# A hybrid decoder layer whose instructions are ordered by the scheduler's timeline model instead of its default estimate

## The chip, the cores and the metric

The kernel runs on one core of a Trainium2 chip. The core has a matmul engine (TensorE; PE in the profile, with its weight loads as a row PEld), a vector engine (DVE), an activation engine (ACT), a general engine (POOL), and a queue that issues the transfers (SP). Each engine takes its instructions strictly in the order in which the program gives them, and an instruction that depends on another engine waits for a semaphore. The metric is device microseconds for one execution; lower is better.

## The reference, cut to what matters

The computation is one layer over x of shape (1, 2048, 1024) in float32, and a final RMSNorm:

```python
h = _rmsnorm(x, norm_w[l])
proj = h @ w_in[l]                       # 8456 columns, split in 13 pieces
y_a = _hgrn2_branch(a_q, a_f, a_i, a_g, lb_all[l], norm_a[l])            # gated linear recurrence, 4 heads
y_b = _gated_deltanet_branch(b_qkv, b_z, b_beta, b_a, conv_w[l], ...)    # delta rule, 4 heads
y_c = _swa_sink_branch(c_q, c_k, c_v, c_g, sinks[l], bias_blk)           # windowed attention, 8 heads
lifted = jnp.einsum('bsnc,ncd->bsnd', ys, w_branch[l])
gates = jax.nn.sigmoid(gate_logits.reshape(Bn, S, N_BRANCHES, D_MODEL))
x = x + jnp.sum(gates * lifted, axis=2) @ w_out[l]
return _rmsnorm(x, final_norm)
```

The delta rule needs, for each chunk, the inverse of a lower triangular matrix with ones on its diagonal (`triangular_solve(eye + A, eye)`), and then carries a 128x128 state from chunk to chunk.

## The kernel before, in words

The sequence is worked through in four blocks of 512 positions (`block(s, ...)`), each with the same program. Two kinds of matmul stand in it.

**Dense matmuls.** Every projection, every lift of a branch and the output projection splits its operands in a high and a low part and makes three matmuls per 128 rows of the contraction: lines 101, 102, 103 (function `mm_ct`, 512 columns each, 24 for one projection, into one of four PSUM banks `ps_d`), or lines 169, 170, 171 (`mm_tc`). Their weights come through `load_w` into four buffers `wHL`: in the first block from the inputs with a split on ACT and DVE (lines 86, 87), later from a copy kept in DRAM (line 82, `wHL<-kept`, 512 KB for twelve matmuls). Dense matmuls of one unit depend little on other units, so they can stand between the small matmuls of another.

**Small matmuls.** Each block has four units A (`unit_a`, lines 402 to 446), four units B (`unit_b`, lines 512 to 645) and four units C (`unit_c`, lines 694 to 732), on the PSUM banks `ps_c0` and `ps_c1`. They are chains: a few small matmuls, then work on DVE, ACT or by DMA on their result, then the next small matmuls. A float32 matmul stands in the trace as two records. In a unit B the chain is:

- line 547: scores of the four chunks, four matmuls in two pairs; DVE makes `NTt` and `QKT` of them (550, 552); ACT copies the diagonal blocks of all four chunks to `NS` (566)
- the inverse of 32 blocks of 16x16, which takes a way through DRAM in both directions:

```python
566  A.copy(NS[r:r + 64], NTt[r:r + 64, :, r:r + 64])
567  nc.sync.dma_start(half(sN, r), NS[r:r + 64])
570  nc.sync.dma_start(L, diag(sN))
574  V.tensor_tensor(t3, ...)                      # 14 steps of two operations on DVE
576  V.tensor_tensor(L[:, 0:j, j + 1:16], ...)
578  nc.sync.dma_start(diag(sX), L)
580  nc.sync.dma_start(XB[r:r + 64], half(sX, r))
581  V.transpose(X[r:r + 64, :, r:r + 64], XB[r:r + 64])
591  T.matmul(yp[...], NS[:, c, :], low(X)[:, c], ...)   # first matmul that needs X
```

- two doublings of the block size (591, 601, each followed by copies and predicated copies on DVE and ACT) and the last one (618, 626)
- the recurrence over four chunks: 635 and 636 read the state; DVE (637); 640; DVE (642); 644 and 645; DVE updates the state (646), on which the next 635 waits.

A unit C has per pair of chunks the scores (694, 696), a softmax on DVE and ACT, transposes (723) and the product with the values (732).

The order in the source is not the order on the engines. Everything is recorded in a `TileContext`, and at its end a list scheduler takes the instructions of all engines one by one, using an estimate of when each is ready, and so fixes the order on every engine and which buffer each tile takes. `issue_after` at a few places adds an edge that keeps an instruction behind another.

## Time and profile before

| | us |
|---|---|
| median of 3 runs | 2517.97 (2510.12 to 2519.35) |
| the profiled execution | 2514.51 |
| span of its core, first to last instruction | 2512.7 |
| PE busy / PEld busy | 2428.6 / 1946.4 |
| DVE / ACT / POOL busy | 1170.9 / 869.2 / 434.2 |
| mean granted TensorE clock | 0.984 |

Times in the trace count from the start of the span. The busy time of PE is the time in which at least one matmul was under way; a matmul's record reaches to the end of its results, so records of neighbours overlap, and the distance from one start to the next tells more than a record's length. "Idle before" names what released an instruction after its engine had stood still.

### The profile page before, as it was taken

To read this page: it belongs to the slowest core of one execution; us is meant where nothing else is said; L and a number is where in the kernel's file an instruction comes from. 1 tells how busy PE (TensorE), PEld (TensorE's weight loads), DVE (VectorE), ACT (ScalarE), POOL (GpSimd) and SP (SyncE) were. 2 spreads that over 40 slices of the span, in tenths; PEclk is the share of its full clock that TensorE was granted. 3 is DMA by queue.
4 is the path that set the end of the run, shared out by engine and by line. 5 is a ranking of instruction groups with operands and counts; after the bars stand their busy time and mean duration, and the time that the engine had idled before them with its cause. 6 is when DMAs were issued, how large, how long until landed. Compare 5 with 4: busy or idle time off the path is not lost. (4 is left out here: it accounts for less than half of the span.)

```text
span 2512.7 us, 37478 instructions
## 1 busy us (share of the span) xinstructions
PE 2428.6 (97%) x13658; PEld 1946.4 (77%) x13658; DVE 1170.9 (47%) x3188; ACT 869.2 (35%) x2288; POOL 434.2 (17%) x821
## 2 busy tenths in 40 slices
PE   8999998999999999899999999989999999998998
PEld 7777776778877777678887877767888787876886
DVE  5666575465345535524214553551322455455321
ACT  5454344444334313323223422332322342233221
POOL 3221011211222101111112210111111221111111
PEclk9999998999999999999999999999999999999999
DMA  7756673769944455264774455425566354442555
GB/s 244 247 193 224 221 260 96 241 221 336 299 134 130 154 161 158 83 208 148 247 218 127 139 156 165 146 88 193 167 228 210 122 155 149 160 150 87 176 193 175
DMA packets 193156, 452.84 MB, mean 180 GB/s; under 512 B 52243, under 2 KB 70588, under 8 KB 192844
## 3 DMA queue, kind: packets, MB, share of 16 engines
q1 hardware_dynamic: 192972, 450.45, 55.3%
q8 instruction: 108, 1.77, 0.3%
q14 instruction: 76, 0.62, 0.1%
HBM read 348.81 MB, written 103.14 MB: 180 GB/s over the span
## 5 line engine op out<-in xcount | busy, mean ns | idle before, releaser
L101 PE MATMUL ps_d<-hH,wHL 128*128 128x512 f32 x1952 | 785.6, 402 | 4.1 <-DVE mm L700 2.2
L102 PE MATMUL ps_d<-hL,wHL 128*128 128x512 f32 x1952 | 783.5, 401 | 0.0
L103 PE MATMUL ps_d<-hH,wHL 128*128 128x512 f32 x1952 | 779.9, 400 | 0.7 <-DVE wHL L87 0.7
L101 PEld LDWEIGHTS ps_d<-hH,wHL 128*128 128x128 f32 x1952 | 369.4, 189 | 77.5 <-DVE mm L700 3.9
L103 PEld LDWEIGHTS ps_d<-hH,wHL 128*128 128x128 f32 x1952 | 369.3, 189 | 71.8 <-issue 1.8
L102 PEld LDWEIGHTS ps_d<-hL,wHL 128*128 128x128 f32 x1952 | 369.4, 189 | 68.0 <-issue 1.7
L87 DVE TENSOR_TENSOR wHL<-wraw,wHL 128x512 fp32r<-128x512 f32 (+1 forms) x194 | 130.6, 677 | 93.3 <-ACT wHL L86 91.2
L362 POOL TENSOR_TENSOR msum<-msum,gth 128x512 f32<-128x512 f32 x64 | 88.6, 1387 | 443.6 <-DVE gth L361 443.6
L101 PE MATMUL ps_d<-yH,wHL 128*128 128x512 f32 x384 | 155.3, 406 | 5.8 <-ACT yH L342 3.7
L86 ACT CAST wHL<-wraw 128x512 fp32r<-128x512 f32 (+1 forms) x194 | 113.7, 590 | 130.9 <-PE ps_d L103 80.8
L103 PE MATMUL ps_d<-yH,wHL 128*128 128x512 f32 x384 | 154.9, 403 | 0.0
L102 PE MATMUL ps_d<-yL,wHL 128*128 128x512 f32 x384 | 153.8, 401 | 0.1
L352 ACT ACTIVATE gth<-ps_d 128x512 f32<-128x512 f32 x96 | 57.3, 597 | 256.9 <-PE ps_d L103 256.1
L361 DVE SCALAR_TENSOR_TENSOR gth<-gth,ps_d 128x512 f32<-128x512 f32 x64 | 43.9, 687 | 184.9 <-PE ps_d L103 177.4
L169 PE MATMUL ps_d<-wHL,mH 128*128 128x512 f32 x256 | 99.7, 391 | 1.3 <-DMA wHL<-kept 1.3
L502 DVE SCALAR_TENSOR_TENSOR qkB<-raw,convw,qkB 128x512 f32<-128x512 f32 x96 | 71.7, 746 | 61.2 <-ACT qkB L500 59.9
L170 PE MATMUL ps_d<-wHL,mH 128*128 128x512 f32 x256 | 99.6, 389 | 0.0
L171 PE MATMUL ps_d<-wHL,mL 128*128 128x512 f32 x256 | 99.5, 389 | 0.0
L101 PEld LDWEIGHTS ps_d<-yH,wHL 128*128 128x128 f32 x384 | 73.0, 191 | 21.8 <-ACT yH L342 4.6
L102 PEld LDWEIGHTS ps_d<-yL,wHL 128*128 128x128 f32 x384 | 73.6, 192 | 15.9 <-DVE yL L343 1.7
L103 PEld LDWEIGHTS ps_d<-yH,wHL 128*128 128x128 f32 x384 | 73.5, 191 | 15.2 <-issue 0.5
L402 PEld LDWEIGHTS ps_c<-qk 128*64 128x64 f32 x1536 | 52.6, 137 | 33.3 <-issue 20.4
(281 smaller groups left out, 3761.0 us busy)
## 6 DMA issues: line engine op xcount, KB each, us to landing
wHL<-kept SPq DMA_DIRECT2D x486, 512.0 KB, 3.6
kept<-wHL SPq DMA_DIRECT2D x162, 512.0 KB, 4.0
wraw<-in_wct_dram SPq DMA_DIRECT2D x122, 256.0 KB, 3.7
wHL<-kept SPq DMA_DIRECT2D x32, 324.0 KB, 4.1
xT<-in_xT_dram SPq DMA_DIRECT2D x32, 256.0 KB, 4.6
xs<-in_x_dram SPq DMA_DIRECT2D x32, 256.0 KB, 4.4
rt<-in_x_dram SPq DMA_DIRECT2D x32, 256.0 KB, 4.6
out_dram<-rt SPq DMA_DIRECT2D x32, 256.0 KB, 4.0
```

Of the source, the lines that this page charges most:

```text
L86: A.copy(w[:, 0, :n], raw[:, :n])
L87: V.tensor_tensor(w[:, 1, :n], raw[:, :n], w[:, 0, :n].bitcast(F32), op=ALU.subtract)
L101: T.matmul(p, wh[:, ks], rh[kt], start=(kt == 0), stop=False)
L102: T.matmul(p, wh[:, ks], rl[kt], start=False, stop=False)
L103: last_mm[0] = T.matmul(p, wl[:, ks], rh[kt], start=False, stop=(kt == nk - 1)).ins
L169: T.matmul(pj[j][:, :n], lh[kt][:, js], wh, start=(kt == 0), stop=False)
L170: T.matmul(pj[j][:, :n], lh[kt][:, js], wl, start=False, stop=False)
L171: T.matmul(pj[j][:, :n], ll[kt][:, js], wh, start=False, stop=(kt == KT - 1))
L352: A.activation(th, gp, AF.Tanh, scale=0.5)
L362: G.tensor_tensor(m, m, th, op=ALU.add)
L402: T.matmul(sp[g * 64:g * 64 + 64, c * 32:(c + 1) * 32], K[:, c * P + g * 64:c * P + g * 64 + 64], qv[:, c, g * nb // 2:(g + 1) * nb // 2, ...
L502: V.scalar_tensor_tensor(dst, raw[:, j:j + TB], convw[:, ti, j:j + 1], dst, op0=ALU.mult, op1=ALU.add)
```

## The change

One argument is added where the context is made:

```diff
-    with tile.TileContext(nc, auto_bufs=True) as tc:
+    with tile.TileContext(nc, auto_bufs=True, schedule_with_timeline_sim=True) as tc:
         _trunk(tc, S, aps, y)
```

No instruction of the computation is added or taken away: both programs have 11,577 matmuls and 1,155 transfers. The scheduler now simulates engines, queues and transfers in time to decide what is ready, and the order on every engine comes out another way. If a run of dense matmuls is one without a small matmul in between, PE has 685 runs before and 334 now.

On PE, in the second block, unit B of head 1. `ps_c1_8551` takes the second pair of score matmuls, `X_8560` is the tile made by the transposes of line 581, `ps_d_...` are dense. Before, from the scores on (89 dense matmuls follow in a row until the first matmul of line 591):

```order
L520 MATMUL ps_c1_8518<-ident_66,vB_8334 128x128 x4
L547 MATMUL ps_c1_8544<-qkB_8333 128x256 x2
L547 MATMUL ps_c1_8551<-qkB_8333 128x256 x2
L102 MATMUL ps_d_8829<-hL_6040,wHL_8830 128x512
L103 MATMUL ps_d_8829<-hH_6039,wHL_8830 128x512
L101 MATMUL ps_d_8829<-hH_6039,wHL_8844 128x512
L102 MATMUL ps_d_8829<-hL_6040,wHL_8844 128x512
```

Now, at the same place:

```order
L103 MATMUL ps_d_9625<-hH_6039,wHL_9640 128x512
L547 MATMUL ps_c1_8551<-qkB_8333 128x256 x2
L591 MATMUL ps_c1_8605<-X_8560,NS_8562 64x64 x4
L601 MATMUL ps_c1_8614<-yb1_507,XB_8563 64x64 x4
L591 MATMUL ps_c1_8625<-X_8560,NS_8562 64x64 x4
L601 MATMUL ps_c1_8634<-yb1_507,XB_8563 64x64 x4
L618 MATMUL ps_c1_8645<-X_8560,NTt_8542 64x64 x4
L626 MATMUL ps_c1_8654<-XB_8563,Y2_8652 64x64 x4
L635 MATMUL ps_c1_8661<-stB1_562,qkB_8333 128x128
```

The dense matmuls that stood between the scores and the first use of the inverse are at other places; between 547 and 591, and between the steps after it, stands nothing. The same holds for the units of heads 1 and 2 in all four blocks: 0 to 5 dense matmuls between 547 and 591, where before there were 89 to 125. For head 0 there are 110 to 133 now (102 to 123 before), and for head 3 there are 52 to 57 and some thirty small ones (66 to 81 before).

On PE, second block, the recurrence of head 2 from its second chunk on. `stB2` is the state, `vn` is made by DVE from the result of 640. Before:

```order
L635 MATMUL ps_c0_9477<-stB2_563,qkB_9131 128x128
L636 MATMUL ps_c0_9477<-stB2_563,qkB_9131 128x128
L102 MATMUL ps_d_9990<-hL_6040,wHL_10005 128x512
L103 MATMUL ps_d_9990<-hH_6039,wHL_10005 128x512
L101 MATMUL ps_d_9990<-hH_6039,wHL_10005 128x512
L640 MATMUL ps_c0_9482<-vB_9132,XT_9356 128x128
L102 MATMUL ps_d_9990<-hL_6040,wHL_10005 128x512
L103 MATMUL ps_d_9990<-hH_6039,wHL_10005 128x512
L101 MATMUL ps_d_10144<-hH_6039,wHL_10145 128x512
L644 MATMUL ps_c0_9486<-vn_9484,KD_9288 128x128
L645 MATMUL ps_c0_9486<-vn_9484,QKT_9341 128x128
```

Now:

```order
L635 MATMUL ps_c0_9477<-stB2_563,qkB_9131 128x128
L636 MATMUL ps_c0_9477<-stB2_563,qkB_9131 128x128
L640 MATMUL ps_c0_9482<-vB_9132,XT_9356 128x128
L644 MATMUL ps_c0_9486<-vn_9484,KD_9288 128x128
L645 MATMUL ps_c0_9486<-vn_9484,QKT_9341 128x128
L635 MATMUL ps_c0_9495<-stB2_563,qkB_9131 128x128
L636 MATMUL ps_c0_9495<-stB2_563,qkB_9131 128x128
L640 MATMUL ps_c0_9500<-vB_9132,XT_9356 128x128
```

Of the 176 steps of this kind in the kernel (636 to 640, 640 to 644, 645 to the next 635), 5 had no dense matmul in between before and 133 had three; now 115 have none, and 46 have ten or more. In unit C, between the scores (694, 696) and the transposes (723) of its 32 pieces, there stood 16 to 26 dense matmuls; now 24 to 42 in 28 of them, and none in the last piece of each block.

On SP, around the transfers of the same inverse as in the first place. `scrN1`, `scrX1` are the DRAM buffers of the way there and back, `wHL<-kept` are weights. Before:

```order
L82 DMA wHL_8892<-kept52_2945 128x1024
L567 DMA scrN1_515<-NS_8562 64x4x64 x2
L82 DMA wHL_8909<-kept53_2967 128x1024
L570 DMA L16_8568<-scrN1_515 32x16x16
L82 DMA wHL_8926<-kept54_2989 128x1024
L82 DMA wHL_8940<-kept55_3008 128x1024
L82 DMA wHL_8957<-kept56_3030 128x1024
L578 DMA scrX1_517<-L16_8568 32x16x16
L82 DMA wHL_8974<-kept57_3052 128x1024
L580 DMA XB_8563<-scrX1_517 64x4x64 x2
```

Now:

```order
L82 DMA wHL_9970<-kept83_4178 128x1024
L567 DMA scrN1_515<-NS_8562 64x4x64 x2
L570 DMA L16_8568<-scrN1_515 32x16x16
L578 DMA scrX1_517<-L16_8568 32x16x16
L580 DMA XB_8563<-scrX1_517 64x4x64 x2
L82 DMA wHL_9991<-kept84_4204 128x1024
```

The weight loads that stood between the four steps of the chain stand before and behind them now.

## Rows read from the trace of the kernel before

**Rows 1.** The page: busy time of each engine, its share of the span, its instructions.

```profile
PE 2428.6 (97%) x13658; PEld 1946.4 (77%) x13658; DVE 1170.9 (47%) x3188; ACT 869.2 (35%) x2288; POOL 434.2 (17%) x821
```

**Rows 2.** The waits of PE: for whom, us in total, times, longest.

```profile
PE ps_c L591 <- DVE X L581: 8.5, 12, 1.4
PE ps_c L723 <- DVE E L716: 3.7, 6, 0.8
```

**Rows 3.** Timeline of PE, head 1, second block: start, length, instruction, [idle before].

```profile
867.39 0.39 PE L103 MATMUL ps_d<-hH,wHL 128*128 128x512 f32 x1
867.62 0.39 PE L101 MATMUL ps_d<-hH,wHL 128*128 128x512 f32 x1
...
868.28 1.89 PE L547 MATMUL ps_c<-qkB 128*128 128x256 f32 x8
...
891.76 0.45 PE L591 MATMUL ps_c<-X,NS 128*64 128x64 f32 x8 [1.39 <-DVE X L581]
...
902.04 0.49 PE L635 MATMUL ps_c<-stB,qkB 128*128 128x128 f32 x2
```

**Rows 4.** Timeline of DVE, ACT and SP between the two matmuls of rows 3.

```profile
871.65 0.83 ACT L566 COPY NS<-NTt 64x256 f32<-64x256 f32 x2 [2.58 <-DVE NTt L550]
872.08 1.25 SPq L567 DMA_DIRECT2D scrN<-NS  x2
875.60 0.33 SPq L570 DMA_DIRECT2D L<-scrN  x1
879.54 0.16 DVE L574 TENSOR_TENSOR L16t<-L 32x14 f32<-32x14 f32 x1 [2.65 <-DMA L<-scrN]
885.59 0.17 DVE L576 TENSOR_TENSOR L<-L,L16t 32x14 f32<-32x14 f32 x1
888.89 12.97 SPq L82 DMA_DIRECT2D wHL<-kept  x4
890.71 0.91 DVE L581 STREAM_TRANSPOSE X<-XB 64x256 f32<-64x256 f32 x2 [4.34 <-DMA XB<-scrX]
```

**Rows 5.** Timeline of PE: the longest (first block) and shortest (third block) such stretch.

```profile
325.38 1.89 PE L547 MATMUL ps_c<-qkB 128*128 128x256 f32 x8
356.88 0.45 PE L591 MATMUL ps_c<-X,NS 128*64 128x64 f32 x8 [0.81 <-DVE X L581]
...
1487.82 1.89 PE L547 MATMUL ps_c<-qkB 128*128 128x256 f32 x8
1509.86 0.45 PE L591 MATMUL ps_c<-X,NS 128*64 128x64 f32 x8
```

**Rows 6.** Timeline of PE, head 3, second block: doublings without dense matmuls.

```profile
1035.98 0.45 PE L591 MATMUL ps_c<-X,NS 128*64 128x64 f32 x8
...
1044.94 0.79 PE L635 MATMUL ps_c<-stB,qkB 128*128 128x128 f32 x2
```

**Rows 7.** Timeline of PE: two steps of the recurrence, head 1 and head 3.

```profile
906.74 0.40 PE L640 MATMUL ps_c<-vB,XT 128*128 128x128 f32 x2
906.89 0.48 PE L101 MATMUL ps_d<-yH,wHL 128*128 128x512 f32 x1
907.20 0.40 PE L102 MATMUL ps_d<-yL,wHL 128*128 128x512 f32 x1
...
907.68 0.39 PE L644 MATMUL ps_c<-vn,KD 128*128 128x128 f32 x2
...
1058.68 0.46 PE L640 MATMUL ps_c<-vB,XT 128*128 128x128 f32 x2
1059.59 0.49 PE L644 MATMUL ps_c<-vn,KD 128*128 128x128 f32 x2 [0.45 <-DVE vn L642]
```

**Rows 8.** Windows: length, busy PE (x), PEld, DVE, ACT, POOL, granted clock, DMA share, GB/s.

```profile
1126.00:1130.40 4.40, 0.00 (x0) 0.00 (x0) 1.25 (x2) 1.30 (x3) 1.82 (x5) 0.99 0.54 200
1130.40:1133.70 3.30, 3.26 (x12) 2.87 (x13) 0.05 (x1) 0.59 (x1) 1.14 (x3) 0.50 0.02 5
1041.60:1048.40 6.80, 5.87 (x29) 4.39 (x29) 4.08 (x12) 2.26 (x5) 0.00 (x0) 0.50 0.01 2
```

## The prediction

> **What bounds the kernel now.** I read the page's engine line first: PE is busy 97% of the span, DVE 47%, ACT 35% [rows 1]. So the time is PE's time, and the change can move it in two ways only: by what PE's matmuls cost in another order, and by how long PE stands still. Next I read the timeline of PE for the real pace. Two dense matmuls in a row start 0.23 us apart (867.39, 867.62), although each record is 0.39 long [rows 3]; prices below go by starts. Then the waits of PE: the list is short, and its entries for the two long chains are small, 8.5 us for the inverse of the delta rule (591 on 581) and 3.7 us for the softmax (723 on 716) [rows 2]. They are small not because these chains are short but because dense matmuls stand in PE's order for as long as each chain takes. The inverse of head 1 in the second block shows it: the scores end at 868.28 + 1.89 = 870.17, the matmul that needs X starts at 891.76 [rows 3], 21.6 us later, and 89 dense matmuls (20.5 us) stand between. What fills that time off PE stands in [rows 4]: DVE and ACT until 872.48 (2.3), the way to DRAM and back until 879.54 (7.1), 28 DVE operations until 885.76 (6.2), the second way until 890.71 (5.0), the transposes (0.9). These steps depend on each other, so no order makes the chain shorter; an order only decides whether PE has other work meanwhile.
>
> **The change part by part.** No instruction is added or removed, so the sum is one of positions. It starts from the profiled execution, 2514.5 us (span 2512.7 and 1.8 around it); the median of the runs is 3.5 above, 0.14%.
>
> 1. Fewer alternations. After a small float32 matmul the first dense one holds PE 0.31 us (906.89 to 907.20 [rows 7]) in place of 0.23, so 0.08 more. Runs of dense matmuls fall from 685 to 334: 351 x 0.08 = -28 us. The other end is 0, if the step were paid elsewhere.
>
> 2. The inverse, heads 1 and 2, four blocks. PE takes its instructions in order, so where 591 stands behind 547, PE waits for the chain. What is queued behind it there is everything else on PE, the dense matmuls too, and through them ACT, DVE and POOL. Eight chains have 0 to 5 dense matmuls in them, 11 in all. 8 x 21.6 - 11 x 0.23 = +170 us. The shortest stretch of this kind lasted 20.1 us (1487.82 + 1.89 to 1509.86), the longest, in the first block, 29.6 (325.38 + 1.89 to 356.88) [rows 5]. I take 21.6, the row of the same head in a later block: with PE still, DVE and ACT have little else to do, which speaks against the long one.
>
> 3. The inverse, head 3. 52 dense matmuls (12 us) and some thirty small ones (at most 0.15 each, from 906.74 to 906.89 [rows 7], 4.5 us) cover 16.5 of 21.6: 4 x 5 = +20. Head 0 has 110 or more, 25 us, and is covered. The 8.5 us that PE waited here before [rows 2] is contained in these figures: -8.5.
>
> 4. The doublings. From 591 to 635 the covered head 1 took 10.3 us (891.76 to 902.04 [rows 3]) with 21 dense matmuls in it (4.8), so 5.5 without them. The bare head 3 took 9.0 (1035.98 to 1044.94 [rows 6]): 3.5 more. Four units were bare, now twelve are: 8 x 3.5 = 28. Head 0 has 105 dense matmuls there now and may lose its remaining waits, which I put at 2 us for each: -8. Together +20.
>
> 5. The recurrence. A bare step from 640 to 644 took 0.91 us (1058.68 to 1059.59); a covered one 0.94 (906.74 to 907.68) of which three dense matmuls are 0.69 [rows 7], so 0.25 of its own. Bare costs 0.66 more. 115 steps are without dense matmuls where 5 were; in eight of them stand eight transposes of another head, cover enough. 102 x 0.66 = +67.
>
> 6. The softmax. It was covered by 16 to 26 dense matmuls, 3.7 to 6.0 us, with 3.7 us of waits in all [rows 2]. The last piece of each block has none now: 4 x 4.7 - 3.7 = +15. In the other 28 pieces the cover has grown.
>
> 7. The clock. After 4.40 us without a matmul PE ran 3.3 us at granted clock 0.50, which is 1.2 GHz, with 12 matmuls; and in a stretch of bare steps it had 0.50 for 6.8 us [rows 8]. A restart of that kind costs half of 3.3: 8 x 1.65 = 13. Bare doublings and bare recurrences are each a stretch like the 6.8 us one, which costs at most 3.4; the doublings' share is already in the 9.0 us of term 4. 12 x 3.4 = 41. I take 54, between 13 (restarts alone) and 95 (both stretches of every unit in full).
>
> The Trainium skill speaks here for less. "TensorE: Matmul & The Clock Gate", section "What's actually happening", says that the array idles at half rate until it is active, as the 0.50 after the wait shows, but advises to put the cost of ramps under 1% of a typical span. That would be at most 25 us for this term, and the sum some 29 lower; a kernel that stops PE dozens of times is not typical, and here the windows decide.
>
> The page "DMA: Bandwidth & Descriptors" of the Trainium skill, section "Anatomy of one DMA", gives a transfer a fixed cost of some 2 us, most of it until the write is confirmed (for the GpSimd path; here SP issues). The four dependent transfers of the chain would be 8 us by it. The rows have 7.1 and 5.0, so 12.1, with the issue between; by the page the sum would be about 8 x 4 = 32 lower. The rows are taken.
>
> Sum: -28 + 170 + 20 - 8.5 + 20 + 67 + 15 + 54 = +309.5; 2514.5 + 309.5 = 2824, say 2825 us. Level steps of units A I cost at nothing: few are bare, and two heads are interleaved there.
>
> **The rivals.**
>
> - Weights come late. In heads 1 and 2 the four steps of the chain now stand together on SP, and no weight load can pass them. For it: SP does hold loads back, 12.97 us for four of them [rows 4]. Against it: they are released when the last step is issued, before 591 can start, and at least 9 us of bare work follow on PE. If the first dense matmuls wait 4 us each time, 8 x 4 = 32 more: 2857.
> - The clock stays at half through every bare stretch. For it: 0.50 for 6.8 us with PE busy 5.87 of them [rows 8]. Against it: bare steps are bound by DVE, not by PE's rate. Term 7 becomes 95: 2865.
> - Empty engines are fast. Every chain takes 20.1, head 3 waits 3.6, and the clock costs restarts alone: 2824 - 12 - 6 - 41 - 10 (two thirds of the gains in terms 4 and 6 doubted) = about 2755.
> - The other side: alternation is what the order before really pays for. It is one mechanism, on PE at each change between dense and small. It would make the kernel faster from the point where a run saves more than (309.5 + 28) / 351 = 0.96 us. The rows show 0.08, and PE's whole stretch from one 640 to its 644, two changes with it, is 0.94. At 1.1 us a run the time would be 2466.
> - The change does nothing that PE feels, 2515: against it stand the orders, which differ on every engine.
>
> **How the numbers follow.** Forecast 0.58, weights 0.12, half clock 0.15, empty engines 0.12, other side 0.02, nothing 0.01. The ends: with 20.1 for the chain and little for the clock, 2745, and I go a little below, to 2735; with a chain of 25.6, half way to the longest, (8 x 4 + 4 x 4 = 48 more), the clock at 95 (41 more) and no gain from term 1, 2941, which I cut to 2930. A difference under 0.5% is about what cannot be told from no change here. Faster 0.02, within 0.5% 0.01, slower 0.97: only the last two rivals are not slower.
>
> **What would show it.** In the profile after: a wait of PE at 591 for DVE's 581 of some 170 to 200 us in all, about twenty microseconds at a time, two in each block; waits at 640, 644 and 635 for DVE of some tens of us; windows without any matmul, each followed by granted clock 0.50, and a mean clock below 0.984; PE busy well under 97%; dense records for the same count at the same pace, with fewer of 0.48 us. If the wait at 591 is under 50 us in all, my reading of the order is wrong; if waits for `wHL<-kept` are large, the first rival was right; if PE is as busy as before and the time is still longer, something dearer than waits was moved.

## The result and the profile after

The changed kernel takes 2832.58 us (median of 4, 2831.27 to 2834.01) against 2518.66 of the kernel before beside it (2510.12 to 2523.98): a ratio of 1.123, 95% interval 1.120 to 1.126. Forecast were 2825 us and a range of 2735 to 2930.

The page of the changed kernel: span, engines, and the granted clock in 40 slices.

```profile
span 2831.5 us, 37513 instructions
...
PE 2512.1 (89%) x13658; PEld 2058.1 (73%) x13658; DVE 1175.8 (42%) x3188; ACT 877.4 (31%) x2292; POOL 448.7 (16%) x821
...
PEclk9999877899999987899999997779999999777999
```

The span is 319 us longer than before and PE is busy 89% of it instead of 97% [rows 1], so most of the difference is PE standing still. PE's busy time also grew, by 83.5 us (2512.1 - 2428.6), with the same 13,658 records; at half clock a record is longer (a small matmul's two records last 0.80 us there and 0.49 at full clock, in the rows of the second experiment below). Four valleys of 7 in the clock's line are the delta rule's units of the four blocks.

The waits of PE after: for whom, us in total, times, longest.

```profile
PE ps_c L591 <- DVE X L581: 161.8, 12, 19.4
PE ps_c L723 <- DVE E L716: 20.0, 8, 4.4
PE ps_c L640 <- DVE vB L637: 18.5, 41, 0.6
PE ps_c L644 <- DVE vn L642: 15.8, 33, 0.5
PE ps_c L635 <- DVE stB L646: 13.8, 29, 0.5
...
PE ps_d L169 <- DMA wHL<-kept: 5.2, 2, 3.0
...
PE ps_d L101 <- DMA wHL<-kept: 1.6, 3, 0.9
```

The first line answers to the 8.5 us of [rows 2]: 161.8 us, up to 19.4 at a time. The softmax (723) went from 3.7 to 20.0, the recurrence (640, 644, 635) waits 48 in 103 steps. The last two lines are all waits of PE for weights from the kept copy, 6.8 us in five; the rival of late weights would have needed them to be large.

The timeline of PE after, unit B of head 1 in the second block.

```profile
1027.55 0.39 PE L103 MATMUL ps_d<-hH,wHL 128*128 128x512 f32 x1
1027.77 1.02 PE L547 MATMUL ps_c<-qkB 128*128 128x256 f32 x4
1046.91 0.70 PE L591 MATMUL ps_c<-X,NS 128*64 128x64 f32 x8 [18.11 <-DVE X L581]
1048.15 1.19 PE L601 MATMUL ps_c<-yb,XB 128*64 128x64 f32 x8 [0.55 <-DVE yb L595]
...
1056.22 0.79 PE L635 MATMUL ps_c<-stB,qkB 128*128 128x128 f32 x2
...
1069.71 0.80 PE L640 MATMUL ps_c<-vB,XT 128*128 128x128 f32 x2 [0.44 <-DVE vB L637]
1070.95 0.80 PE L644 MATMUL ps_c<-vn,KD 128*128 128x128 f32 x2 [0.44 <-DVE vn L642]
```

The dense matmuls end where the scores begin, and after the scores PE stands still for 18.11 us; in [rows 3] dense matmuls filled that time. From 591 to 635 pass 9.3 us without a dense matmul. The step from 640 to 644 at the end takes 1.24 us, against 0.94 with three dense matmuls in it before, of which 0.25 was its own [rows 7].

What fills the 18.11 us off PE, on ACT, SP's queue and DVE.

```profile
1030.41 0.81 ACT L566 COPY NS<-NTt 64x256 f32<-64x256 f32 x2
1033.57 0.33 SPq L570 DMA_DIRECT2D L<-scrN  x1
1035.41 0.16 DVE L574 TENSOR_TENSOR L16t<-L 32x14 f32<-32x14 f32 x1 [5.45 <-DMA L<-scrN]
1041.44 0.17 DVE L576 TENSOR_TENSOR L<-L,L16t 32x14 f32<-32x14 f32 x1
1045.63 0.44 DVE L581 STREAM_TRANSPOSE X<-XB 64x256 f32<-64x256 f32 x1 [4.02 <-DMA XB<-scrX]
```

These rows answer to [rows 4]. ACT ends at 1031.22; the way to DRAM and back lasts 4.2 us (to 1035.41) instead of 7.1; DVE's steps take the same 6.2 (to 1041.61); the second way takes 4.0 instead of 5.0.

Windows of the same stretch: length, busy PE (x), PEld, DVE, ACT, POOL, granted clock, DMA share, GB/s.

```profile
1028.00:1047.00 19.00, 0.89 (x6) 0.49 (x6) 7.31 (x35) 1.97 (x6) 1.19 (x1) 0.61 0.20 53
1047.00:1056.00 9.00, 6.29 (x48) 4.61 (x48) 5.29 (x18) 2.44 (x8) 0.53 (x1) 0.50 0.01 2
1056.00:1080.00 24.00, 20.72 (x90) 17.04 (x89) 10.99 (x25) 7.48 (x20) 3.31 (x9) 0.78 0.15 48
```

Behind the wait PE runs at granted 0.50 through the doublings, and at 0.78 on the mean through the recurrence. Over the whole span 494 us lie at 0.50 in 33 stretches, against 84 in 14 before.

For the comparisons below I worked out one more figure from all records of each trace: the own time of the units B. It is the time from the end of the scores to 591 (chain), from 591 to 635 (doublings) and from the first 635 to the last 645 (recurrence), less 0.2265 us for each dense matmul inside, summed over the 16 units. "Half-clock dense" is what dense matmuls that follow each other lost at granted 0.50, by the same pace. "Runs" are uninterrupted runs of dense matmuls.

| us | time | chain | doublings | recurrence | sum | half-clock dense | runs |
|---|---|---|---|---|---|---|---|
| before | 2519 | 49 | 100 | 108 | 257 | 13 | 685 |
| changed | 2833 | 193 | 126 | 215 | 534 | 44 | 334 |
| bare inverse | 2723 | 209 | 129 | 134 | 473 | 20 | 605 |
| bare units | 2842 | 210 | 137 | 231 | 578 | 18 | 461 |
| moved cover, timeline | 2801 | 131 | 126 | 248 | 505 | 45 | 318 |
| pieces, timeline | 2734 | 94 | 100 | 239 | 433 | 19 | 314 |
| pieces, default | 2538 | 32 | 109 | 138 | 279 | 3 | 611 |
| moved cover, default | 2473 | 38 | 101 | 100 | 238 | 8 | 720 |

The changed kernel's units cost 277 us more than before and its dense matmuls 31. The two columns overlap: of the half-clock dense 20 us lie inside the units, 19 of them in the recurrences, and stand in the own times too; before it was 3. So 17 of the 31 are counted twice, and together it is 277 + 31 - 17 = 291 us of the 319 between the two spans. Counted like this, the other rows come within 36 us of the difference between their span and that of the kernel before.

### The profile page after: what moved, and what is told of

The parts are those of the page before. It is cut to its first block, busy times and chain, and to the rows that moved or that the text cites. A ratio compares the mean times of both kernels' runs of the same rounds, so it can differ in the third digit from the quotient of the medians.

```text
span 2831.5 us, 37513 instructions
## 1 busy us (share of the span) xinstructions
PE 2512.1 (89%) x13658; PEld 2058.1 (73%) x13658; DVE 1175.8 (42%) x3188; ACT 877.4 (31%) x2292; POOL 448.7 (16%) x821
## 4 chain that ended last, share of the span: by engine, by line
PE 79%; DVE 7%; DMA 7%; ACT 3%; issue 2%; POOL 1%; SPq 1%; ACTq 0%; DVEq 0%; POOLq 0%
PE ps_d L101 19%; PE ps_d L103 18%; PE ps_d L102 18%; PE ps_d L169 2%; PE ps_d L170 2%; PE ps_d L171 2%; PE ps_c L402 2%; PE ps_c L732 1%; PE ps_c L640 1%; PE ps_c L635 1%; DMA XB<-scrX 1%; PE ps_c L644 1%; DVE L16t L574 1%; DVE L L576 1%; DMA wHL<-kept 1%
## 5 line engine op out<-in xcount | busy, mean ns | idle before, releaser
L591 PE MATMUL ps_c<-X,NS 128*64 128x64 f32 x256 | 24.8, 296 | 169.5 <-DVE X L581 161.8
L591 PEld LDWEIGHTS ps_c<-X,NS 128*64 128x64 f32 x256 | 17.7, 186 | 180.4 <-issue 166.6
L242 POOL TENSOR_TENSOR soB<-soB,eq 128x1 f32<-128x1 f32 x64 | 13.2, 207 | 515.2 <-ACT junkB L649 515.0
L101 PEld LDWEIGHTS ps_d<-yH,wHL 128*128 128x128 f32 x384 | 75.2, 199 | 25.2 <-ACT yH L106 6.3
L102 PEld LDWEIGHTS ps_d<-yL,wHL 128*128 128x128 f32 x384 | 76.5, 199 | 17.5 <-DVE yL L343 1.7
```

The lines of the kernel that those rows point to most:

```text
L101: T.matmul(p, wh[:, ks], rh[kt], start=(kt == 0), stop=False)
L102: T.matmul(p, wh[:, ks], rl[kt], start=False, stop=False)
```

## The experiments

My theory: PE executes in order, dense matmuls between the small ones of a unit B are its only cover, and the new order takes them out. Rivals: the clock, dear alternations between dense and small, the order on SP's queue.

**Only the inverse of heads 1 and 2 made bare, default estimate.** Dense matmuls recorded later are kept behind the first 591 of these heads:

```diff
+                        m591 = T.matmul(yp[...], NS[:, c, :], low(X)[:, c], ...).ins
+                    if lv == 4 and h in (1, 2):
+                        hold[0] = m591
 ...
+                with held():        # tc.issue_after(hold[0])
                     T.matmul(p, wh[:, ks], rh[kt], start=(kt == 0), stop=False)
```

> The default order, with one thing taken from it: dense matmuls recorded after unit B of heads 1 and 2 may not stand ahead of the first matmul at line 591 of that unit, so the eight inverse chains of these heads are bare, as the timeline order has them. Head 0 loses its cover in the doublings and the recurrence with it; runs of dense matmuls are 605 (685 before, 334 in the changed kernel). Theory (PE's lost cover is the price): 8 x 18.7, the bare chain as the changed kernel's trace has it, = +150; head 0 bare in four doublings (4 x 3.5) and recurrences (4 x 5.6) = +36; clock +15 to +25; 80 runs fewer, -6. About 2515 + 195 = 2710 (2670 to 2740), with 140 to 160 us of waiting at 591 for the transposes. Rival 1 (the timeline order is slow for its clock above all, the chain's wait is paid back by shorter work afterwards): under 2600. Rival 2 (the queue for transfers, in the order that only the timeline model makes): no more than 2560, since that order isn't here.

Measured: 2722.83 us, ratio 1.080 (1.076 to 1.084), 199.5 above before, inside the theory's 2670 to 2740. The wait of PE (591 and 581 are 596 and 586 here):

```profile
PE ps_c L596 <- DVE X L586: 176.0, 12, 20.1
```

The wait came back, in the default order, with 160 us more of chain in the table. So neither the timeline order on SP nor the number of runs is needed for the loss.

**Heads 1 and 2 bare through the recurrence.** The same, with `hold[0] = m645` at `c == NT - 1`.

> As the run with the bare inverse, but the dense matmuls are held until the last matmul at line 645 of heads 1 and 2, so that eight doublings and eight recurrences are bare too; 461 runs of dense matmuls. Theory: against the bare inverse +8 x 3.5 (doublings) + 8 x 5.6 (recurrence) = +73, clock +15 to +25, 144 runs fewer -12: +75 to +90, so about 2790, near the changed kernel although the scheduler's estimate is the default one. Rival 1 (only the inverse counts; a bare recurrence costs nothing because the dense matmuls cost the same wherever they stand): +0 to +15 against the bare inverse. Rival 2 (alternations are dear): faster than the bare inverse.

Measured: 2841.95 us, 1.127 (1.122 to 1.131): 119 more than the bare inverse, not 75 to 90, and as slow as the changed kernel, under the default estimate. Two steps from 640 to 644 (645 and 649 here), head 0 and then head 1 of the second block:

```profile
935.66 0.49 PE L645 MATMUL ps_c<-vB,XT 128*128 128x128 f32 x2 [0.44 <-DVE vB L642]
936.59 0.49 PE L649 MATMUL ps_c<-vn,KD 128*128 128x128 f32 x2 [0.44 <-DVE vn L647]
...
984.56 0.80 PE L645 MATMUL ps_c<-vB,XT 128*128 128x128 f32 x2 [0.44 <-DVE vB L642]
985.80 0.80 PE L649 MATMUL ps_c<-vn,KD 128*128 128x128 f32 x2 [0.45 <-DVE vn L647]
```

And the windows of head 1's doublings and recurrence:

```profile
968.80:978.10 9.30, 6.58 (x48) 4.83 (x48) 4.59 (x17) 1.63 (x6) 0.53 (x1) 0.50 0.00 0
978.10:996.00 17.90, 12.60 (x42) 9.45 (x41) 4.86 (x15) 2.67 (x10) 2.54 (x7) 0.50 0.00 0
```

A bare step is 0.93 us in the first and 1.24 in the second. A whole bare recurrence took 17.5 us with all of it at granted 0.50, and 14.8 with 8.0 us at 0.50 (head 0, second block), by the records of this trace. I had put the eight recurrences at 5.6 us each; the table gives 97 us for all of them, and that is the miss.

**The pieces: cover given back by hand, under either estimate.** Unit B is split behind 581; the 192 dense matmuls of the first branch's lift are cut in three pieces, each held between 547 and 591 of heads 1, 2 and 3:

```diff
-        f1 = unit_b(1)
-        merge(0, yA)
+        g1 = first(1)             # unit B up to 581
+        cover(yA, range(0, 3))    # lift, held behind the last 547
+        f1 = rest(g1)             # 591 held behind the piece
```

> The changed kernel (timeline estimate), but the 192 dense matmuls of the first branch's lift are cut in three pieces, and each piece is held between the scores and 591 of head 1, 2 and 3: their chains, doublings and recurrences get cover (108 or more, 76 to 96 dense matmuls), head 0 loses all of its own. 314 runs of dense matmuls, as few as in the changed kernel. Theory: of the wait at 591, 162 us, the four chains of head 0 stay (4 x 19 = 76), -86; doublings -8 x 3.5 = -28; recurrence bare in 4 units instead of 14, -50; clock -20 to -35: about 2832 - 190 = 2640 (2600 to 2720). Rival 1 (weights and transfers in the timeline's order on SP, or the alternations, set the time): 2800 or more. Rival 2 (the pieces are only moved, and are missed as cover where they stood): 2800 or more, with new waits of PE in the softmax or in the level steps.

> The same source as the covered timeline run (the lift in three pieces, held in the chains of heads 1, 2, 3), but with the default estimate. Cover by position: chains of all heads (89 or more), doublings 20 to 24 and recurrences 26 to 40 in heads 1 to 3; bare are the doublings and recurrences of head 0 alone. 611 runs of dense matmuls (314 there). Theory: it is the position of the dense matmuls, not their number of runs, that sets the time: head 0 costs +15 in doublings and +40 in the recurrence against the kernel before, heads 1 to 3 give back 30 to 50, clock +10 to +15: 2545 (2525 to 2590), 150 to 200 faster than the same source under the timeline estimate although it alternates twice as often. Rival (pieces held in the chains are what made that run slow): 2700 or more.

Measured: 2734.36 us (1.084, 1.080 to 1.088) with the timeline estimate, 2538.44 (1.005, 1.003 to 1.007) with the default one. The waits of PE in the first (599 is 591, 652 is 644):

```profile
PE ps_c L599 <- DVE X L586: 89.2, 4, 23.9
PE ps_c L652 <- DVE vn L650: 23.8, 52, 0.5
```

The first wait is down to head 0's four chains, as expected, but the fall was 98 us and not 190. The scheduler put 76 to 96 dense matmuls in a doubling that needs 20, and none in the recurrences of heads 0 to 2, which I had not read off the order; the table's 239 in that column is the miss. With the default estimate the same source is 196 us faster, 7 from the time expected, with almost twice the runs. What counts is where the cover stands.

**Four chains covered, nothing else meant.** The kernel of the last experiment below, under the timeline estimate:

```diff
-    with tile.TileContext(nc, auto_bufs=True) as tc:
+    with tile.TileContext(nc, auto_bufs=True, schedule_with_timeline_sim=True) as tc:
```

> The recorded order of the moved cover (two tiles of the lift after unit B of head 3) under the timeline estimate. Against the changed kernel it differs in one thing that counts: the four chains of head 2 now have 97 to 101 dense matmuls in them; the chains of head 1, the doublings and most of the recurrence steps stay bare as they were; 318 runs of dense matmuls. Theory: four bare chains fewer, 4 x 18.4 = -74, and the clock behind them -5 to -10: 2832 - 80 = 2752 (2740 to 2775). Rival (what the chain no longer waits for is paid elsewhere): 2800 or more. Rival (the recorded order is what matters, not the estimate): under 2600.

Measured: 2800.54 us, 1.110 (1.107 to 1.114), so 32 less than the changed kernel, not 80. The chain fell by 62 as expected. But the recurrence rose by 33: in the later blocks heads 0 and 1 have some 93 and 20 dense matmuls there now where 168 and 44 stood. The cover was not added but moved; my sum had left out the place that it came from.

**The clock, four times.** Dense matmuls on operands that lie ready, whose results nobody uses, are put into bare places, so that only the clock could gain. First 64 in each of the eight chains:

```diff
+            if h in (1, 2):
+                heat = bank(ct)
+                for _ in range(64):
+                    T.matmul(heat, hH[0][:, 0:P], hH[0], start=True, stop=True)
```

> The changed kernel with 64 additional dense matmuls on operands that lie ready (their results are not used) between the scores and 591 of heads 1 and 2, in each of the eight bare chains: 64 x 0.228 = 14.6 us of work inside a wait of 18 to 19 us. The chain is not shorter, so the time changes by the clock alone: the doublings and dense matmuls behind these chains run at full clock. Theory: of the 494 us at granted 0.50 about half lies behind these chains; the price of the clock is 50 us in all, so 20 to 40 us faster than the changed kernel, 2795 to 2812, and the wait at 591 for the transposes falls from 162 to 50 us without that being a gain. Rival (the clock costs nothing, since bare stretches are bound by the vector engine): 2825 to 2840. Rival (the clock is the main price of the change): under 2750.

Measured: 2841.39 us, 1.126 (1.122 to 1.130): no gain. Windows of one heated chain, of the rest of its wait, and of the doublings behind it:

```profile
1033.00:1047.00 14.00, 14.00 (x63) 11.34 (x61) 6.06 (x32) 1.57 (x5) 0.00 (x0) 1.00 0.17 49
1047.00:1050.20 3.20, 0.13 (x1) 0.02 (x1) 0.88 (x2) 0.00 (x0) 0.00 (x0) 1.00 0.18 41
1050.50:1064.00 13.50, 10.80 (x64) 8.71 (x60) 8.20 (x24) 4.24 (x11) 0.53 (x1) 0.50 0.00 1
```

The inserted matmuls end at 1047, PE then waits 3.2 us, and the doublings run at 0.50 all the same. The run says nothing of the price; the heat ended too early.

Then 78 in the chain and two of 256 columns after each small group of the doublings and the recurrence, in free columns of the same bank:

```diff
+            def warm(t, n, m):        # n matmuls on tile t, kept behind m; heads 1 to 3
 ...
+                        m = T.matmul(t[:, 256:512], hH[0][:, 0:P], hH[0][:, 0:256], ...).ins
 ...
+                    m = warm(r2, 2, T.matmul(r2[:, 0:P], XT[:, c, :], VR[:, c, :], ...).ins)
```

> The changed kernel with additional dense matmuls on ready operands in all bare places of units B, their results not used: 78 of 512 columns in the chains of heads 1 and 2 (17.7 of 18 to 19 us), and two of 256 columns after each small group of the doublings and of the recurrence in heads 1 to 3. Nothing is shortened by them but what hangs on the clock. Theory: bare recurrences of the runs so far lasted 13.7 us with 3.8 us at granted 0.50, 18.3 us with 18.3, so 0.31 us per us at half clock; 12 units with some 10 us at half give -37; 163 more dense matmuls at half clock than before, 0.19 each, give -31; the inserted matmuls cost some +10 where they are late: 2832 - 58 = 2775 (2755 to 2800). Rival (bare steps cost what they cost at any clock; the heated chains without gain speak for it): 2825 to 2860. Rival (the clock is most of the loss): under 2700.

Measured: 2880.92 us, 1.141 (1.138 to 1.145), 48 slower than the changed kernel. DVE's waits name the inserted line, 562, for the state update and for `vn`:

```profile
DVE stB L667 <- PE ps_c L562: 74.5, 45, 5.6
...
DVE vn L662 <- PE ps_c L562: 54.2, 44, 5.4
```

The readers of a step waited for the inserted matmuls, which write the tile that they read. A bad experiment. Written to the bank of the step before, they don't:

```diff
-                    m = warm(r2, 2, T.matmul(r2[:, 0:P], XT[:, c, :], VR[:, c, :], ...).ins)
+                    m = warm(rb, 2, T.matmul(r2[:, 0:P], XT[:, c, :], VR[:, c, :], ...).ins)
```

> As the heated units, but the inserted matmuls of the doublings and of the recurrence write into the bank of the step before, so that the vector engine's and the activation engine's reads no longer wait for them (in the heated units the trace named the inserted line as what DVE waited for, 74.5 us at the state update alone). The steps measured alone kept 0.87 us at granted 1.00 with two such matmuls in each gap and fell to 1.17 without. The scheduler also puts 27 dense matmuls into the doublings of head 3 (0 to 9 in the changed kernel). Theory (the clock costs what the steps alone show): recurrence -37, dense matmuls at half clock -31, head 3's doublings -10: 2832 - 78 = 2755 (2740 to 2790). Rival (the clock costs little in this kernel): 2815 to 2835. Rival (inserted matmuls are late in any place): above 2840.

Measured: 2825.06 us, 1.120 (1.117 to 1.124). By the own times the recurrence fell by 26 and half-clock dense by 16, but the doublings rose by 15 and the chains by 18. The gain is there and the inserted work costs nearly as much. So last only the recurrence, with the other inserted matmuls taken out:

```diff
-                for _ in range(78):
-                    T.matmul(heat, hH[0][:, 0:P], hH[0], start=True, stop=True)
 ...
-                    m = warm(heat, 2, m)
```

> The changed kernel with nothing added but two dense matmuls of 256 columns (not used) in each gap of the recurrence of heads 1 to 3, written to the bank of the step before; chains and doublings are left as they are, and dense matmuls stand where they stood but for some 20 that go to head 1's recurrence. It tells the price of the clock in one place, where the last but one heated version mixed it with what the inserted matmuls cost in the doublings (+15) and behind the chains (+18). Theory: the recurrence goes from 215 to about 187 us over the sixteen units, as there, and the dense matmuls behind it run at full clock, -16 to -25: 2832 - 45 = 2788 (2775 to 2805). Rival (the clock is worth nothing at the end, what it gives is waited for elsewhere): 2820 to 2840.

Measured: 2812.16 us, 1.115 (1.106 to 1.124), 20 faster than the changed kernel. Half-clock dense fell from 44 to 24 us, by 17 of these 20 outside the units; the recurrence fell by 6 only, and the chains rose by 10. About 20 us of the loss were given back by the clock; the 45 that I expected did not come.

**The steps measured alone.** A kernel of five stretches and nothing of the layer, run once; each matmul is kept behind the one before (`m`, `w`, `r` are operands made of x):

```diff
+        # A4: four dense, one small
+        for i in range(24):
+            for k in range(4):
+                pe(d, w, r)
+            pe(c[:, 0:P], m, m)
 ...
+        # B: bare steps
 ...
+        for i in range(24):
+            e = bank("e")
+            pe(e[:, 0:P], m, vn)
+            vn = sb.tile([P, P], F32, name="vnB", tag="vn")
+            V.tensor_scalar(vn, e[:, 0:P], 0.5, None, op0=ALU.mult)
```

> A kernel that computes nothing of the layer (it writes zeros): five stretches, three times over. G: 96 dense matmuls of 512 columns, then 24 small float32 ones. A4: 24 times four dense and one small. B: 24 bare steps, a small matmul and a vector operation that depend on each other. H: the same with two dense matmuls of 256 columns behind each small one. C: the same with three dense ones of 512 columns. Theory: G 0.23 per dense matmul and 0.14 to 0.15 per small one; A4 0.08 more per group than the sum of its parts, 1.13 in all; B about 0.83 a step at granted 1.00 and 1.08 at 0.50, falling to 0.50 within the stretch; H at the pace of B's fast steps with granted 1.00 throughout; C 0.94. Rival (a change between the two kinds is dear): A4 1.5 or more. Rival (the clock doesn't matter to a bare step): B at one pace throughout.

Its timeline of PE: 24 small matmuls in a group (two records each), alternation of four dense and one small, bare steps early and late, steps with two dense matmuls of 256 columns, steps with three of 512.

```profile
28.53 5.52 PE L62 MATMUL ps_c<-m 128*128 128x128 f32 x48
33.80 1.17 PE L62 MATMUL ps_d<-hH 128*128 128x512 f32 x4
34.81 0.38 PE L62 MATMUL ps_c<-m 128*128 128x128 f32 x2
34.95 1.18 PE L62 MATMUL ps_d<-hH 128*128 128x512 f32 x4
...
74.03 0.49 PE L62 MATMUL ps_e<-vnB,m 128*128 128x128 f32 x2 [0.38 <-DVE vnB L101]
74.90 0.49 PE L62 MATMUL ps_e<-vnB,m 128*128 128x128 f32 x2 [0.38 <-DVE vnB L101]
...
86.95 0.80 PE L62 MATMUL ps_e<-vnB,m 128*128 128x128 f32 x2 [0.38 <-DVE vnB L101]
88.13 0.79 PE L62 MATMUL ps_e<-vnB,m 128*128 128x128 f32 x2 [0.38 <-DVE vnB L101]
...
113.03 0.49 PE L62 MATMUL ps_e<-vnH,m 128*128 128x128 f32 x2
113.90 0.49 PE L62 MATMUL ps_e<-vnH,m 128*128 128x128 f32 x2
...
142.85 0.38 PE L62 MATMUL ps_e<-vnC,m 128*128 128x128 f32 x2
143.78 0.38 PE L62 MATMUL ps_e<-vnC,m 128*128 128x128 f32 x2
```

Windows of the bare steps (first 5 us and after) and of those with two dense matmuls each:

```profile
72.40:77.40 5.00, 2.76 (x13) 1.61 (x11) 1.68 (x6) 0.00 (x0) 0.00 (x0) 1.00 0.01 3
77.40:98.00 20.60, 13.98 (x36) 8.97 (x37) 5.00 (x18) 0.00 (x0) 0.00 (x0) 0.50 0.00 0
110.50:130.70 20.20, 16.84 (x95) 12.12 (x94) 6.69 (x23) 0.00 (x0) 0.00 (x0) 1.00 0.01 1
```

Alternating, four dense and one small take 1.15 us. Grouped, the small ones stand 0.22 apart (33.80 - 28.53 over 24), so the same work is 4 x 0.227 + 0.22 = 1.13. An alternation costs 0.02, not 0.08: what the dense matmul loses behind a small one, small ones lose behind each other. A bare step is 0.87 at granted 1.00 and 1.18 at 0.50, which came 5 us into the stretch. With three dense matmuls a step is 0.93, 0.25 of it its own (0.93 - 3 x 0.227): lost cover is worth 0.62 us a step at full clock and 0.93 at half.

**A better version.** If a little cover in each chain is what counts, head 3, bare in its doublings before [rows 6], is the place to mend:

```diff
-        merge(0, yA)
+        merge(0, yA, range(0, 6))
 ...
         f3 = unit_b(3)
+        merge(0, yA, range(6, KT))
```

> Default estimate, as in the kernel before; of the first branch's lift (eight output tiles of 24 dense matmuls) the last two tiles are recorded after unit B of head 3 instead of before unit B of head 2. Heads 0 to 2 keep their cover; head 3, whose doublings were bare (0 or 4 dense matmuls), gets 19 to 21 there and 31 instead of 24 in the recurrence. Theory (cover in the doublings and in the recurrence is what counts, and little of it is enough): own time of head 3's doublings 33 -> 24 us and of its recurrence 41 -> 28 us over the four blocks, clock -5, 35 runs more +3: about -24, so 2495 (2480 to 2510). Rival (cover taken from elsewhere is missed there): 2515 to 2530.

Measured with the default estimate: 2473.00 us against 2521.96, ratio 0.980 (0.977 to 0.983), faster than both kernels and than the 2480 to 2510 expected; the interval lies on both sides of 0.98, so whether the gain is a full 2% is not settled. Its page and PE's wait at 591:

```profile
span 2474.8 us, 37465 instructions
...
PE 2416.8 (98%) x13658; PEld 1935.5 (78%) x13658; DVE 1166.2 (47%) x3188; ACT 868.2 (35%) x2288; POOL 436.3 (18%) x821
...
PEclk9999999999999999999999989999999999999999
```

```profile
PE ps_c L591 <- DVE X L581: 10.2, 11, 1.7
```

PE is busy 98%, and 52 us lie at granted 0.50 instead of 84. It has more runs (720) than any other kernel here, and is the fastest. Of the 38 us between the spans of the two traces the own times account for 19 and half-clock dense for 5; the rest I did not place. More was possible: head 0's doublings in the third block have their 22 dense matmuls, but took 17.3 us at granted 0.53, with PE busy all the time, where the kernel before (second row) took 10.5 at 1.00.

```profile
1437.70:1455.00 17.30, 17.30 (x71) 10.37 (x71) 5.31 (x18) 4.01 (x10) 0.53 (x1) 0.53 0.16 60
1460.00:1470.50 10.50, 10.31 (x69) 6.43 (x70) 5.27 (x19) 3.38 (x9) 0.53 (x1) 1.00 0.31 100
```

## Why the prediction was right

The mechanism and the places were right: the bare chains, two in each block of about twenty microseconds, the waits in the recurrence, half clock behind them, next to no waits for weights. Of the sizes, step by step:

- Step 1, alternations, -28: should have been its other end, about 0. The slots from a dense matmul to a small one did shrink, by some 35 us (waits left out, beyond 0.2265 each), but small ones that follow each other are slower than the 0.15 that I read, and the steps alone gave 0.02 a run, 7 us for 351 runs. Also, 208 of the 351 lie inside the doublings (92) and the recurrences (116). Steps 4 and 5 were priced from rows of whole stretches, which contain the alternations, so there step 1 counted the same gain twice.
- Steps 2 and 3, the chains, +170, +20 and -8.5: too much. They cost +144. The eight bare chains lasted 18.0 to 19.4 us, below the 20.1 of [rows 5] that I took for the lower end. The rows of before were no bound: the two ways to DRAM took 8.2 us now instead of 12.1, at DMA shares of 0.21 and 0.17 instead of 0.71 and 0.64. I put that to the weight loads that ran beside them before. It was not tried by itself, but a chain of the bare inverse agrees: in head 1 of the second block no weight load is issued during the chain there either, under the default estimate, and the two ways took 4.3 and 4.2 us. The Trainium skill's "DMA: Bandwidth & Descriptors", section "Anatomy of one DMA", would have had 8 us for four, by an estimate from its 2 us each; here the page was nearer than the covered rows: by it these terms would have been 32 lower, 149.5, and 144 were measured.
- Step 4, the doublings, +20: +26; a bare one took 9.3 us against 9.0.
- Step 5, the recurrence, +67: 103 bare steps, as counted, but 0.98 us each on the mean instead of 0.91. The whole column rose by 107, which contains what step 7 had put there.
- Step 6, the softmax, +15: its wait rose by 16.
- Step 7, the clock, +54: half-clock dense alone is 31. Of the recurrence's 107, 40 are beyond step 5. Of these, 17 are the half-clock dense matmuls inside the recurrences, which the 31 contain already; in the other 23 the clock has a part, since a bare step is 0.93 at granted 1.00 and 1.24 at 0.50. So the term is between 31 and 54, inside my 13 to 95, and the forecast stands at its upper end. Steps 5 and 7 together were put at 67 + 54 = 121, and 107 + 31 - 17 = 121 were measured. The last heated run gave back 20; how the 23 divide the experiments leave open. The Trainium skill's "TensorE: Matmul & The Clock Gate", section "What's actually happening", had made it at most 25, by an estimate from its 1%: the half-clock dense matmuls alone exceed that.

The measured parts, without step 1, are 144 + 26 + 107 + 16 + 31 - 17 = 307, against 319 between the two spans; the other 12 I did not place, and no gain of 28 is left over in them. The forecast of 309.5 came as near as it did partly by luck, because errors cancelled: chains 37 too dear against a gain of 28 that was not there. The rival of late weights fell with 6.8 us of waiting. The rival of half clock throughout was 32 too high in time, and too dear in its term, 95 against 54 at most: in the windows above the recurrence has 0.78 on the mean. The rival of empty engines was nearer on the chains, which were shorter even than its 20.1, but had restarts alone for the clock and was 78 too low. The other side, 0.96 us per alternation, fell to 0.02.

## What to carry to other kernels

On an engine that executes in order and is the bound, what matters is how much independent work stands inside each dependent chain, not how often the kinds of work alternate: count it per chain, in the places it is taken from as well. In these kernels a little everywhere (20 dense matmuls in a doubling, 30 in a recurrence) beat much in one place. A duration read from a covered stretch may contain what the cover's own transfers cost it (here argued, not tried by itself); bare, the same chain can be shorter: 18.0 to 19.4 us for the eight chains here, where the shortest covered one had 20.1.

## What was unexpected of the hardware

The issue of `L<-scrN` to the first step on its data took 1.8 us (1033.57 to 1035.41) with the weight loads away, 3.9 with them [rows 4]. In the steps measured alone the granted clock was 1.00 through the dense matmuls and the first 5 us of bare steps, then 0.50 until dense matmuls had come again; with two dense matmuls of 256 columns in each gap it stayed at 1.00 for all 24 steps, and they cost nothing (0.87 us a step either way). In the heated chains 3.2 us of waiting behind 14 us of dense matmuls were followed by granted 0.50. And cover did not always keep the clock: in the last kernel a wait of 1.7 us was followed by 17.3 us at 0.53 in which PE was busy throughout.
